# A DiT block on one NeuronCore: SiLU and gating of all attention pairs done in the output stage

## The chip, the core and the metric

One NeuronCore of a Trainium2 chip runs the whole program. The metric is device time in microseconds (us) of one execution; the time of a kernel is the median of its runs. A profile is one further execution taken with the hardware profiler; its times are counted from the start of the span. Engines are named as in the profile: PE (TensorE, matrix products), PEld (its weight loads), DVE (VectorE), ACT (ScalarE), POOL (GpSimd), SP (SyncE, which here only issues DMAs). ACT and POOL issue DMAs as well, each from its own queue and in its own instruction order.

## The reference, cut to what matters

One transformer layer on 1024 tokens of width 1024, with 256 context tokens. After an adaLN-modulated RMS norm, one projection gives eight groups of 512 columns. Half of the mixing width is attention, half a gated short convolution:

```python
q, k, v, za, u, bg, cg, zc = split(h @ w_in)
attn = neighbourhood_attention(q, k, v, kc, vc, rpb) * silu(za)
conv = bg * conv3(cg * u) * silu(zc)
x_new = x + gate * (concat([attn, conv]) @ w_out)
```

Attention has 8 heads of 64, here 4 pairs of heads with 128 channels each. Softmax is over a local window plus all context keys, so each head's output has to be divided by its row sums.

## The kernel before, in words

Everything is float32. To keep its precision, each product is done as three passes on high and low parts (`mm3`: high x high, high x low, low x high); each operand is split by a copy to the rounded type on ACT and a subtraction on DVE.

**Layout.** The mixed activations are kept with channels on partitions: eight blocks `f` of 128 channels by 1024 tokens. Blocks 0 to 3 are the attention pairs, 4 to 7 the convolution groups. Each goes through DRAM, in halves of 512 tokens (256 KB each).

**Stages.** (1) Norms and the first convolution group, to some 100 us. (2) The projections of q, k and v, to some 270 us. (3) Attention, to some 540 us: 36 steps (`quarter(n)`, four for a head), pipelined over each other. Into each step the generator `fill` puts two to four ticks of six products each, from the remaining projection units: first the units of `za` (`attn_group(f)`, one for each pair), then the convolution groups 1 to 3. The units' products are the rows `pu` of the profile. (4) The output stage, from 553 us: eight blocks times two halves of `w_out`, for eight tiles of 128 tokens; its products are the rows `pout`.

**Order.** In stage 3 the order of every engine's compute instructions and of the DMAs of SP is as written (`strict`, `behind`, L49 to L60); work that is put off is kept in two lists (`chore`, L301) and taken up at fixed places in the step. In stage 4 a scheduler orders the instructions of each engine. Engines take their instructions strictly in order, DMA issues too, so an issue that waits holds up what is behind it on that engine. A DMA issued by ACT or SP signals on one of eight completion counters, taken in turn by both, and it waits until the last transfer on its counter has landed.

**One attention step.** PE turns the running maxima (`pmx<-ci,mx`), DVE reduces them (`rm`), PE spreads the result (`pmx<-ci,rm`), ACT copies it (`mg`). PE does the scores of a new step (`pss`, `pc`). DVE subtracts the maxima, ACT takes two exponentials of each part (`phc`, `sc`, `phl`, `sb`), POOL and DVE form the low parts (`plc` on POOL, `pll` on DVE), PE multiplies by the values (`po`). DVE also adds the bias and updates the maxima (`mx`).

**SiLU and gate of a pair, before.** When both halves of the unit of `za` are done, `attn_group` has ACT take the SiLU of both out of PSUM, tile `zs` (`silus`, L477), and SP store them to `zs_d`. ACT's exponential and its SiLU need different tables, so ACT loads a table ahead of the two SiLUs and another ahead of the next exponential. When a pair's second head is done, its row sums and output lie in DRAM (`rs_d`, `o_d`; `finish`, L1035). For pairs 0 to 2, `gated(p)` (L1263) then advances by one piece in each step (L1081): SP loads the sums, DVE inverts them, SP stores them (`ri_d`); then for each half SP loads SiLU (`zs`), output (`tb`) and inverse sums (`rb`, two loads, each repeated over 64 partitions), DVE multiplies `zs` by `rb`, in a later step `tb` by `zs`, and SP stores the product to `y_d`. Pair 3 ends too late for that: `recip` (L498) inverts its sums and the output stage does its gate.

**Output stage, before.** For the blocks in the order `FORDER` = 4, 5, 6, 0, 1, 2, 3, 7, `put_y` loads `y_d` half by half, tile `tb` (four buffers of tag `zt`), and splits it: `yh` on ACT, `yl` on DVE. For block 3 it loads `zs` and `tb`, and two `rb` from POOL's queue, and does the two multiplications first. `load_wo` loads a half of a block of `w_out` (`woraw`, two buffers) and splits it into `woh` and `wol`. All these loads but `rb` are issued by ACT. PE first runs the six token tiles 0 to 5 of the first half of `w_out` through the blocks in turn, then the other tiles. `out_tile` multiplies by the gate (DVE), adds `x` (POOL) and stores.

Of the kernel before, what the change touches and what calls it, by code (L numbers as in the profile page):

```python
# [10 lines left out]
F32 = mybir.dt.float32  # L11
F32R = mybir.dt.float32r
BF16 = mybir.dt.bfloat16
AF = mybir.ActivationFunctionType
ALU = mybir.AluOpType
# [4 lines left out]
P = 128  # L20
D = 1024
T = 1024
# [5 lines left out]
NPAIR = NH // 2  # L28
NEG = -1.0e30
CTXT = 3  # L30
FORDER = [4, 5, 6, 0, 1, 2, 3, 7]
# [8 lines left out]
def body(tc, es, x, ctxt, w_ada, b_ada, w_in, q_g, k_g, rpbr, w_out, vecs, cst, out):  # L40
# [21 lines left out]
    pe, act, dve, pool = every = [ordered(e) for e in (nc.tensor, nc.scalar, nc.vector, nc.gpsimd)]  # L62
    sp = ordered(nc.sync)

    def sbuf(name, side=None, bufs=1):
        kw = {} if side is None else {"side": side}
        return tc.tile_pool(name=name, bufs=bufs, reuse_waits="tile", **kw)

    def psum(name):
        return tc.tile_pool(name=name, bufs=1, space=PSUM, reuse_waits="tile")  # L70
# [19 lines left out]
    def many(name, n, shape):  # L90
        return [dr.tile(shape, F32, name=f"{name}{i}")[:] for i in range(n)]
# [4 lines left out]
    o_d = many("o_d", NPAIR, [P, T])  # L96
    y_d = many("y_d", KT, [P, T])
    g_d = dr.tile([1, D], F32, name="g_d")
    rope_d = dr.tile([P, 2048], F32, name="rope_d")
    rs_d = many("rs_d", NPAIR, [2, 2, 512])  # L100
    zs_d = many("zs_d", NPAIR, [P, T])


    q_d = many("q_d", NH, [2, HD, 4, 2, 256])
# [46 lines left out]
    cvp = hs.enter_context(sbuf("cvp", side="right"))  # L151
# [149 lines left out]
    def chore(on_act=None, on_dve=None, queue=soon, frees=None):  # L301
        queue.append([on_act, on_dve, frees])
        if act not in strict:
            do_acts()
            do_dves()

    def do_acts():
        for c in soon + (slow if not any(c[1] and c[1].__name__ == "product" for c in soon) else []):
            if c[0]:
                c[0]()  # L310
                c[0] = None

    def do_dves(most=99):
        for queue in chores:
            while queue and not queue[0][0] and (queue is soon or most > 0 and not soon):
                on_dve = queue.pop(0)[1]
                if on_dve:
                    on_dve()
                    most -= 1
# [18 lines left out]
    def unit(col):  # L338

        w = ahead.pop(col, None)  # L340
        if w is None:
            w = []
            for r in loaded.pop(col, None) or unit_load(col):
                unit_split(r, w)
        nxt = follows.get(col)
        for half in range(2):
            cols = slice(half * 512, (half + 1) * 512)
            for k in range(KT):
                if k % 2 == 0:
                    yield None  # L350
                if k == 0:
                    while any(c[2] == half for c in slow):
                        do_acts()
                        do_dves()
                    ps = psm.tile([P, 512], F32, name="pu", tag="U", bufs=2)
                if k % 2 == 0:
                    tick = 4 * half + k // 2
                    if nxt and tick == 0:
                        raws = unit_load(nxt)
                    if nxt and tick in (3, 5):  # L360
                        unit_split(raws[tick // 5], ahead.setdefault(nxt, []))
                mm3(ps, *w[k], hh[k][:, cols], hl[k][:, cols], k == 0, k == KT - 1)
            yield half, ps

    def blocked(v):
        return v.rearrange("p (b r c) -> p b r c", b=4, r=16)

    def by_row(v):
        return v.rearrange("p (r b c) -> p b r c", r=16, b=4)
# [11 lines left out]
    def z_col(f):  # L381
        return CZA + f * P if f < 4 else CZC + (f - 4) * P
# [94 lines left out]
    def silus(z):  # L477
        out = []
        for half, ps in z:
            out.append(cvp.tile([P, 512], F32, name="zs", tag="ub", bufs=2))  # L480
            act.activation(out[half], ps, AF.Silu)
        return out

    def attn_group(f):

        z = []
        for got in unit(z_col(f)):
            if got:
                z.append(got)
            else:  # L490
                yield

        def on_act():
            for half, zs in enumerate(silus(z)):
                sp.dma_start(zs_d[f][:, half * 512:(half + 1) * 512], zs)
        chore(on_act)

    def recip(p, pl):  # L498

# [5 lines left out]
    def load_sums(f, half, rb, queue):  # L505
        for i in range(2):
            queue.dma_start(rb[64 * i:64 * i + 64],
                            ri_d[f][i:i + 1, half * 512:(half + 1) * 512].broadcast_to([64, 512]))
# [658 lines left out]
    for n in range(NT + 3):  # L1167


        p, t = divmod(n, NB)  # L1170
# [89 lines left out]

    gating = []

    def gated(f):  # L1263

        ri = ap.tile([P, 16], F32, name="ri", tag="ri", bufs=4)
        sp.dma_start(ri, rs_d[f].rearrange("h b (x c) -> (h b x) c", c=16))
        yield
        dve.reciprocal(ri, ri)
        sp.dma_start(ri_d[f].rearrange("h (x c) -> (h x) c", c=16), ri)
        yield  # L1270
        for half in range(2):
            cols = slice(half * 512, (half + 1) * 512)
            zs, tb, rb = (ap.tile([P, 512], F32, name=n, tag=n, bufs=1) for n in ("zs", "tb", "rb"))
            sp.dma_start(zs, zs_d[f][:, cols])
            sp.dma_start(tb, o_d[f][:, cols])
            load_sums(f, half, rb, sp)
            yield
            dve.tensor_tensor(zs, zs, rb, ALU.mult)
            yield
            dve.tensor_tensor(tb, tb, zs, ALU.mult)  # L1280
            sp.dma_start(y_d[f][:, cols], tb)

    with sbuf("att") as ap, psum("psb") as psb:
        sbank = psb.tile([P, 2, 512], F32, name="pss")
        strict[:] = every
        mx = ap.tile([P, T], F32, name="mx")
        sb_new = lambda: ap.tile([P, 2, 384], F32, name="sb", tag="sb", bufs=3)
        mg = ap.tile([P, T], F32, name="mg")
        heads[0].load_v()
        for n in range(4 * NH + 4):  # L1290
            h, g = divmod(n, 4)
            if 0 < h < NH and g == 0:
                heads[h].load_v()
            if h + 1 < NH and g:
                nx = heads[h + 1]
                for load in ((nx.masks, nx.load_q), (nx.load_k,), ())[g - 1]:
                    load()
            quarter(n)
            if ready:
                p = ready.pop()  # L1300
                if p < NPAIR - 1:
                    gating[:] = [gated(p)]
                else:
                    recip(p, ap)
        for _ in fill:
            do_dves()
            do_acts()
        while soon or slow:
            do_dves()
            do_acts()  # L1310
        strict[:] = []
# [5 lines left out]
    op = es.enter_context(sbuf("op"))  # L1317
# [2 lines left out]

    def load_wo(wp, nh, f):
        raw = op.tile([P, 512], F32, name="woraw", tag="woraw", bufs=2)
        act.dma_start(raw, w_out[0, f * P:(f + 1) * P, nh * 512:(nh + 1) * 512])
        wh = wp.tile([P, 512], F32R, name=f"woh{nh}{f}")
        wl = wp.tile([P, 512], F32R, name=f"wol{nh}{f}")
        act.copy(wh, raw)
        dve.tensor_tensor(wl, raw, wh[:].bitcast(F32), ALU.subtract)
        wo[nh, f] = wh, wl

    def put_y(yp, f):  # L1330

        yh = yp.tile([P, T], F32R, name=f"yh{f}")
        yl = yp.tile([P, T], F32R, name=f"yl{f}")
        for half in range(2):
            cols = slice(half * 512, (half + 1) * 512)
            tb = op.tile([P, 512], F32, name="tb", tag="zt", bufs=4)
            if f == NPAIR - 1:
                zs = op.tile([P, 512], F32, name="zs", tag="zt", bufs=4)
                rb = op.tile([P, 512], F32, name="rb", tag="rb", bufs=2)
                act.dma_start(zs, zs_d[f][:, cols])  # L1340
                act.dma_start(tb, o_d[f][:, cols])
                load_sums(f, half, rb, pool)
                dve.tensor_tensor(zs, zs, rb, ALU.mult)
                dve.tensor_tensor(tb, tb, zs, ALU.mult)
            else:
                act.dma_start(tb, y_d[f][:, cols])
            tv = blocked(tb[:]) if f < NPAIR else by_row(tb[:])
            act.copy(natural(yh[:], half), tv)
            dve.tensor_tensor(natural(yl[:], half), tv, natural(yh[:].bitcast(F32), half), ALU.subtract)
        y[f] = yh, yl  # L1350

    for f in FORDER[:-1]:
        put_y(op, f)
        load_wo(op, 0, f)
# [28 lines left out]
    for n, (nh, t) in enumerate([(0, 6), (0, 7)] + [(1, t) for t in range(NB)]):  # L1383
        ps = bank("pout", "US"[n % 2])
# [54 lines left out]
```

## Time and profile before

| | |
|---|---|
| median of 3 runs | 645.64 us (645.0 to 645.97) |
| the profiled execution: its time / its span | 646.57 us / 644.8 us |
| granted TensorE clock | 1.00 |
| PE busy, DVE busy, ACT busy, POOL busy | 98%, 67%, 50%, 20% of the span |
| bytes moved by DMA | 125.46 MB, mean 195 GB/s |
| DVE busy from 375 to 415 us | 37.25 of 40 us |
| PE busy from 544 to 584 us | 40.00 of 40 us |

A busy PE is not a PE at its peak here: matrix products overlap and their ends are modelled, so a wait of a few tenths of a us hides in a busy figure. Waits are read off the starts of successive products instead. Times in the views are us from the start of the span; a row of a timeline has start, length, engine, line, operation, tile written <- tiles read, and in brackets the idle time ahead of it with what ended it. L55 is the line of the helper that records ordered instructions, so these are told apart by their tiles.

### The profile page before, as it was taken

The page shows a single profiled execution, that of the slowest core. Times are in us where ns is not written, and L with a number is a line of the kernel's source. Part 1 is how long each engine was busy: PE and PEld are TensorE (multiplying, and loading weights), DVE is VectorE, ACT ScalarE, POOL GpSimd, SP SyncE. Part 2 cuts the span into 40 slices and gives each one's busy share as a digit, 9 for nine tenths or more (in the row PEclk, how much of TensorE's full clock was granted, in tenths as well). Part 3 has the DMA queues.
Part 4 walks back from the last instruction along what each step waited for, and adds up shares of the span by engine and source line. Part 5 has one row for each costly group of instructions (what it writes and reads, how often), then busy time and mean ns, then how long its engine had stood idle before and what let it go on. Part 6 is the DMA issues. An engine that isn't in the chain of part 4 may idle for free.

```text
span 644.8 us, 10300 instructions
## 1 busy us (share of the span) xinstructions
PE 629.4 (98%) x3479; PEld 537.3 (83%) x3480; DVE 432.9 (67%) x819; ACT 322.2 (50%) x692; POOL 130.3 (20%) x138
## 2 busy tenths in 40 slices
PE   8899999999999999999999999999999999999997
PEld 3477798999899999877878888888888888888885
DVE  1677746865775846557787889988998864575111
ACT  3666725533534543438776658565675545352000
POOL 1205003313223231102121111121111111004421
PEclk9999999999999999999999999999999999999999
DMA  8962556778795998799947768886872224976621
GB/s 325 374 227 104 134 186 196 213 219 233 215 278 148 279 267 236 194 236 216 230 114 209 188 149 204 209 211 154 220 166 76 79 79 118 307 236 206 199 98 53
DMA packets 118864, 125.46 MB, mean 195 GB/s; under 512 B 32817, under 2 KB 89353, under 8 KB 117532
## 3 DMA queue, kind: packets, MB, share of 16 engines
q1 hardware_dynamic: 112348, 113.23, 61.7%
q10 hardware_dynamic: 6208, 11.05, 5.8%
q0 software_dynamic: 256, 0.54, 0.3%
q8 instruction: 27, 0.44, 0.3%
q14 instruction: 25, 0.20, 0.1%
HBM read 88.01 MB, written 38.53 MB: 196 GB/s over the span
## 4 chain that ended last, share of the span: by engine, by line
PE 68%; DMA 9%; DVE 8%; ACT 6%; SPq 5%; issue 2%; POOL 2%; ACTq 0%; DVEq 0%; POOLq 0%
PE pu L55 18%; PE pacc L55 17%; PE po L55 5%; PE pout L76 5%; PE pout L75 5%; PE pout L74 4%; DMA v<-v_d 3%; DMA k_s<-k_d 3%; PE tr L55 3%; SPq L55 3%; PE cacc L55 3%; DVE mx L55 2%; PE acc L55 2%; PE pss L55 2%; PE pmx L55 2%
## 5 line engine op out<-in xcount | busy, mean ns | idle before, releaser
L55 PE MATMUL pu<-h,uh 128*128 128x512 f32 x544 | 169.0, 392 | 0.0
L55 PE MATMUL pacc<-wh,h 128*128 128x384 f32 x512 | 135.5, 338 | 0.0
L55 PEld LDWEIGHTS pu<-h,uh 128*128 128x128 f32 x544 | 98.2, 188 | 17.0
L55 PE MATMUL pu<-h,ul 128*128 128x512 f32 x272 | 106.4, 391 | 0.0
L55 PEld LDWEIGHTS pacc<-wh,h 128*128 128x128 f32 x512 | 92.8, 188 | 0.4 <-ACT qn L55 0.4
L55 POOL TENSOR_TENSOR plc<-sc,phc 128x512 fp32r<-128x512 f32 x32 | 42.5, 1330 | 221.1 <-ACT sc L55 99.2
L55 PE MATMUL pacc<-wl,h 128*128 128x384 f32 x256 | 85.6, 334 | 0.0
L55 POOL TENSOR_TENSOR ss<-ss,few 128x4 f32<-128x4 f32 (+1 forms) x40 | 41.9, 1050 | 127.8 <-DVE ss L55 127.4
L55 PEld LDWEIGHTS pu<-h,ul 128*128 128x128 f32 x272 | 51.1, 188 | 11.3
L55 DVE TENSOR_TENSOR mx<-mx,sb 128x384 f32<-128x384 f32 (+1 forms) x64 | 55.6, 877 | 2.0
L75 PE MATMUL pout<-wol,yh 128*128 128x512 f32 x128 | 49.8, 389 | 0.0
L76 PE MATMUL pout<-woh,yl 128*128 128x512 f32 x128 | 49.6, 389 | 0.0
L74 PE MATMUL pout<-woh,yh 128*128 128x512 f32 x128 | 48.3, 389 | 0.0
L55 PEld LDWEIGHTS pacc<-wl,h 128*128 128x128 f32 x256 | 48.1, 188 | 0.1
L55 DVE TENSOR_REDUCE ss<-sq 128x4 f32<-128x260 f32 (+1 forms) x40 | 15.8, 394 | 46.3 <-ACT sq L55 46.3
L55 ACT COPY mg<-pmx 128x256 f32<-128x256 f32 x32 | 12.0, 374 | 58.0 <-PE pmx L55 44.7
L55 ACT ACTIVATE sq<-pacc 128x256 f32<-128x256 f32 x32 | 12.3, 385 | 52.7 <-PE pacc L55 51.8
L1371 DVE TENSOR_TENSOR ot<-pout,gate 128x512 f32<-128x512 f32 x16 | 10.9, 689 | 38.3 <-PE pout L76 36.2
L55 DVE TENSOR_TENSOR pll<-sb,phl 128x768 fp32r<-128x768 f32 (+2 forms) x33 | 29.3, 889 | 7.6 <-ACT sb L55 7.6
L1372 POOL TENSOR_TENSOR ot<-ot,xr 128x512 f32<-128x512 f32 x15 | 20.1, 1351 | 67.9 <-DVE ot L1371 66.5
L55 DVE TENSOR_TENSOR sc<-sc,mg 128x512 f32<-128x512 f32 x32 | 21.8, 683 | 17.5 <-ACT mg L55 17.5
L55 ACT ACTIVATE qn<-pacc,ss 128x64 f32<-128x64 f32 x128 | 30.0, 329 | 6.3 <-POOL ss L55 3.2
(151 smaller groups left out, 1275.9 us busy)
## 6 DMA issues: line engine op xcount, KB each, us to landing
uraw<-in_w_in SPq DMA_DIRECT2D x34, 256.0 KB
q_d<-qs SPq DMA_DIRECT2D x64, 128.0 KB
k_s<-k_d SPq DMA_DIRECT2D x16, 512.0 KB
q_s<-q_d SPq DMA_DIRECT2D x32, 256.0 KB
wr<-in_w_in SPq DMA_DIRECT2D x40, 192.0 KB
slab<-in_w_ada SPq DMA_DIRECT2D x6, 1024.0 KB
t_d<-btw SPq DMA_DIRECT2D x8, 576.0 KB
bt<-t_d SPq DMA_DIRECT2D x8, 576.0 KB
```

Source lines behind the costliest of these rows:

```text
L55: i = emit(*a, **kw)
L74: i = pe.matmul(ps, ah, bh, start=first, stop=False)
L75: pe.matmul(ps, ah, bl, start=False, stop=False)
L76: pe.matmul(ps, al, bh, start=False, stop=last)
L1371: dve.tensor_tensor(ot, ps, gate[:, cols], ALU.mult)
L1372: (dve if (nh, t) == (1, NB - 1) else pool).tensor_tensor(ot, ot, xr, ALU.add)
```

## The change

`attn_group` no longer takes the SiLU: ACT copies each half of `za` out of PSUM as soon as it is done, and SP stores it raw to `z_d`. `gated` becomes `inverse`, which only inverts the sums of pairs 0 to 2. In the output stage `put_y` now treats all four pairs alike: it loads `z_d`, `o_d` and the inverse sums, ACT takes the SiLU in SBUF, DVE does the two multiplications, and then the split follows as before. The inverse sums of all pairs are loaded from POOL's queue, through two buffers. The tag `zt` has six buffers instead of four. The loads of blocks 1, 2, 3 and 7, and of their part of the first half of `w_out`, are issued by SP instead of ACT. `y_d` is now used by the convolution groups alone.

```diff
     def attn_group(f):
-        z = []
+        def keep(half, ps):
+            z = cvp.tile([P, 512], F32, name="z", tag="ub", bufs=2)
+            act.copy(z, ps)
+            sp.dma_start(z_d[f][:, half * 512:(half + 1) * 512], z)
+
         for got in unit(z_col(f)):
             if got:
-                z.append(got)
+                chore(lambda got=got: keep(*got))
             else:
                 yield
-
-        def on_act():
-            for half, zs in enumerate(silus(z)):
-                sp.dma_start(zs_d[f][:, half * 512:(half + 1) * 512], zs)
-        chore(on_act)
...
-    def gated(f):
+    def inverse(f):
         ri = ap.tile([P, 16], F32, name="ri", tag="ri", bufs=4)
         sp.dma_start(ri, rs_d[f].rearrange("h b (x c) -> (h b x) c", c=16))
         yield
         dve.reciprocal(ri, ri)
         sp.dma_start(ri_d[f].rearrange("h (x c) -> (h x) c", c=16), ri)
-        yield
-        for half in range(2):
-            cols = slice(half * 512, (half + 1) * 512)
-            zs, tb, rb = (ap.tile([P, 512], F32, name=n, tag=n, bufs=1) for n in ("zs", "tb", "rb"))
-            sp.dma_start(zs, zs_d[f][:, cols])
-            sp.dma_start(tb, o_d[f][:, cols])
-            load_sums(f, half, rb, sp)
-            yield
-            dve.tensor_tensor(zs, zs, rb, ALU.mult)
-            yield
-            dve.tensor_tensor(tb, tb, zs, ALU.mult)
-            sp.dma_start(y_d[f][:, cols], tb)
...
     def load_wo(wp, nh, f):
         raw = op.tile([P, 512], F32, name="woraw", tag="woraw", bufs=2)
-        act.dma_start(raw, w_out[0, f * P:(f + 1) * P, nh * 512:(nh + 1) * 512])
+        (act if nh or f in FORDER[:4] else sp).dma_start(raw, w_out[0, f * P:(f + 1) * P, nh * 512:(nh + 1) * 512])
...
     def put_y(yp, f):
...
-            tb = op.tile([P, 512], F32, name="tb", tag="zt", bufs=4)
-            if f == NPAIR - 1:
-                zs = op.tile([P, 512], F32, name="zs", tag="zt", bufs=4)
+            tb = op.tile([P, 512], F32, name="tb", tag="zt", bufs=6)
+            queue = act if f in FORDER[:4] else sp
+            if f < NPAIR:
+                zs = op.tile([P, 512], F32, name="zs", tag="zt", bufs=6)
                 rb = op.tile([P, 512], F32, name="rb", tag="rb", bufs=2)
-                act.dma_start(zs, zs_d[f][:, cols])
-                act.dma_start(tb, o_d[f][:, cols])
+                queue.dma_start(zs, z_d[f][:, cols])
+                queue.dma_start(tb, o_d[f][:, cols])
                 load_sums(f, half, rb, pool)
+                act.activation(zs, zs, AF.Silu)
                 dve.tensor_tensor(zs, zs, rb, ALU.mult)
                 dve.tensor_tensor(tb, tb, zs, ALU.mult)
             else:
-                act.dma_start(tb, y_d[f][:, cols])
+                queue.dma_start(tb, y_d[f][:, cols])
```

In the built programs, the instructions of PE, DVE and POOL up to the output stage stand in the same order, without the twelve multiplications on DVE. ACT has six table loads fewer (7 instead of 13) and, for each pair, a copy at two places where two SiLUs stood at one. In the output stage the scheduler gives another order: on PE a seventh token tile, and later an eighth, now stand among the products of the first six.

More of the change, by code (lines that the diff above doesn't have):

```diff
@@ L100, in body @@
     rs_d = many("rs_d", NPAIR, [2, 2, 512])
-    zs_d = many("zs_d", NPAIR, [P, T])
+    z_d = many("z_d", NPAIR, [P, T])
     q_d = many("q_d", NH, [2, HD, 4, 2, 256])
@@ L1301, in body @@
                 if p < NPAIR - 1:
-                    gating[:] = [gated(p)]
+                    gating[:] = [inverse(p)]
                 else:
```

## The prediction

> **What bounds the kernel now.** I read the page first, then the chain of waits, the timeline of PE around the steps that the chain names, and the table of windows for the output stage.
>
> ```profile
> span 644.8 us, 10300 instructions
> ...
> PE 629.4 (98%) x3479; PEld 537.3 (83%) x3480; DVE 432.9 (67%) x819; ACT 322.2 (50%) x692; POOL 130.3 (20%) x138
> ```
>
> PE is the bound: every other engine has idle time, and the kernel can only gain where PE waits. The change touches two stages, the attention (some 275 to 540 us) and the output stage (553 us to the end), so I ask where PE waits in the first, and whether it would wait in the second. In the chain, pieces of other engines stand between PE's where it waited:
>
> ```profile
> 318.78 1.28 ACT L55
> ...
> 392.44 0.68 DVE tb L55
> ...
> 553.28 1.59 PE pout L74 x7
> ```
>
> The first is a table load ahead of an exponential, the second one of the gating multiplications; both go. The third gives PE's pace in the output stage: 1.59 / 7 = 0.227 us for one product.
>
> **Part 1: what the attention gets back.** First a step in which nothing was late, then five in which something was:
>
> ```profile
> 467.02 0.39 PE L55 MATMUL pu<-h,ul 128*128 128x512 f32 x1
> 467.25 0.38 PE L55 MATMUL pmx<-ci,mx 128*128 128x128 f32 x2
> 467.39 0.48 PE L55 MATMUL po<-phc,v 128*65 128x256 f32 x2
> 467.70 0.28 PE L55 MATMUL po<-plc,v 128*65 128x256 f32 x1
> ...
> 468.06 0.28 PE L55 MATMUL po<-plc,v 128*65 128x256 f32 x1
> 468.17 0.41 PE L55 MATMUL pmx<-ci,rm 128*128 128x128 f32 x2
> ```
>
> ```profile
> 298.71 0.27 PE L55 MATMUL pmx<-ci,mx 128*128 128x128 f32 x1
> ...
> 299.71 0.48 PE L55 MATMUL po<-phc,v 128*65 128x256 f32 x2
> ...
> 300.38 0.28 PE L55 MATMUL po<-plc,v 128*65 128x256 f32 x1
> 300.83 0.43 PE L55 MATMUL pmx<-ci,rm 128*128 128x128 f32 x2 [0.17 <-DVE rm L55]
> ...
> 322.21 0.47 PE L55 MATMUL po<-phc,v 128*65 128x256 f32 x2
> 323.24 0.34 PE L55 MATMUL po<-plc,v 128*65 128x256 f32 x1 [0.57 <-POOL plc L55]
> ...
> 323.65 0.28 PE L55 MATMUL po<-plc,v 128*65 128x256 f32 x1
> 324.13 0.43 PE L55 MATMUL pmx<-ci,rm 128*128 128x128 f32 x2 [0.20 <-DVE rm L55]
> ...
> 345.39 0.28 PE L55 MATMUL po<-plc,v 128*65 128x256 f32 x1
> 345.84 0.43 PE L55 MATMUL pmx<-ci,rm 128*128 128x128 f32 x2 [0.17 <-DVE rm L55]
> ...
> 396.72 0.39 PE L55 MATMUL pu<-h,ul 128*128 128x512 f32 x1
> 397.25 0.41 PE L55 MATMUL pmx<-ci,mx 128*128 128x128 f32 x2
> ...
> 474.75 0.27 PE L55 MATMUL pmx<-ci,mx 128*128 128x128 f32 x1
> ...
> 475.29 0.47 PE L55 MATMUL po<-phc,v 128*65 128x256 f32 x2
> ```
>
> Read start to start. Undisturbed, the two `pmx` take 467.39 - 467.25 = 0.14, `po<-phc` to `po<-plc` 0.31, the last `plc` to `pmx<-ci,rm` 0.11, `pu` to `pmx` 0.23. So PE lost 1.00 - 0.14 = 0.86 at 298.7, 0.45 - 0.11 = 0.34 at 300.4, 1.03 - 0.31 = 0.72 at 322.2, 0.48 - 0.11 = 0.37 at 323.7, 0.45 - 0.11 = 0.34 at 345.4: together 2.63 us. These lie in the steps behind the three pairs' SiLUs that fall in the attention:
>
> ```profile
> L55 ACT ACT_TABLE_LOAD x13 | 16.7, 1283 | 1.0 <-PEq L1422 0.7
> ```
>
> ```profile
> L55 ACT ACTIVATE zs<-pu x16: 592/597/644, 130.6 to 542.4; 128x512 f32<-128x512 f32 x16
> ```
>
> Six loads of 1.28 go, 7.7 us of ACT, two around each pair. The SiLU itself only becomes a copy of the same 512 columns, which I cost at nothing. The load at 318.78 made the exponentials, and so `plc`, 1.28 later, more than the 0.72 lost there; at 298.7 the load ahead of the SiLUs delayed `mg`, and DVE's chain from it, by some 1.0 (an estimate: the load less the shift of one copy), more than 0.86. The other three are `rm` behind a late `pll` on the same chains.
>
> The remaining two, 0.53 - 0.23 = 0.30 at 396.7 and 0.54 - 0.14 = 0.40 at 474.8, wait for DVE's `mx`, and on DVE a gating multiplication stood 4 to 5 us earlier in the same step (392.44 above is one):
>
> ```profile
> L55 DVE TENSOR_TENSOR tb<-tb,zs 128x512 f32<-128x512 f32 x6 | 4.1, 685 | 0.0
> L55 DVE TENSOR_TENSOR zs<-zs,rb 128x512 f32<-128x512 f32 x6 | 4.1, 683 | 0.0
> ```
>
> Each that goes makes `mx` some 0.6 to 0.7 earlier. That gives 0.70 us, and the whole comes to 2.63 + 0.70 = 3.3 us. Two still smaller waits of the kind may come on top (0.4 at most, an estimate), and what is late next may take some back: with ACT and DVE ahead, `po` can wait for the loads of `v` and `k`, which issue no sooner than PE frees their buffers. The bounds are 1.6 (half) and 3.9; I take 3.3. All else there is free: SP has 30 DMAs fewer, the stores of `z_d` are as many and as large as those of `zs_d`, and the shorter hold of PSUM can only help.
>
> **Part 2: what the output stage has to do more.** It has all the work that left: 6 more SiLUs on ACT (6 x 0.60 = 3.6 us; the table is already SiLU's from the last convolution group), 12 more multiplications on DVE (8.2 us), 6 more loads of 256 KB, 12 more `rb` loads of 128 KB on POOL's queue, issued while POOL is idle.
>
> ```profile
> 544.00:560.00 16.00, 16.00 (x72) 13.23 (x72) 9.16 (x15) 5.84 (x10) 2.09 (x4) 1.00 1.00 321
> 560.00:568.00 8.00, 8.00 (x37) 6.64 (x36) 4.60 (x7) 4.65 (x9) 0.00 (x0) 1.00 0.84 275
> 568.00:576.00 8.00, 8.00 (x37) 6.61 (x36) 5.82 (x10) 2.85 (x5) 0.00 (x0) 1.00 0.76 231
> 576.00:584.00 8.00, 8.00 (x37) 6.62 (x36) 4.08 (x7) 3.63 (x7) 0.00 (x0) 1.00 0.47 146
> ```
>
> ```profile
> 578.29 0.69 DVE L1349 TENSOR_TENSOR yl<-tb,yh 128x512 fp32r<-128x512 f32 x1 [0.27 <-ACT yh L1348]
> ```
>
> After the stretch and its length stand the busy times of PE, PEld, DVE, ACT and POOL, the clock, the DMA share and GB/s. PE never waits here before the change. DVE has 23.7 of 40 us, ACT 17.0: there is room for 8.2 and 3.6. But the DMA is full, share 1.00, from 544 to 560; the last `yl` is ready at 579.0.
>
> *By bytes.* In the order of the changed program, 47 units of 256 KB are asked for from 542 up to pair 3's last load of `o_d` (9 for blocks 4, 5, 6 with their `w_out`, 7 for each of the four pairs, `rb` and `w_out` included, 7 for the gate row, the last convolution stores and `x`, 3 for block 7 and the second half of `w_out`). At 321 GB/s a unit takes 0.82: 544 + 47 x 0.82 = 582.5. At 275, for all that comes after 560 (27.4 units x 0.95), it is 586.1. PE's first product that needs pair 3 has 133 of the stage ahead of it, since the scheduler put two further tiles among the first six (before, it is 110): 553.3 + 133 x 0.227 = 583.5. From the landing to `yh` there are a multiplication and a copy, some 1.5 us with hand-overs. So PE waits 582.5 + 1.5 - 583.5 = 0.5 to 4.1 us, middle 2.3.
>
> The Trainium skill (DMA: Bandwidth & Descriptors, Issuing engines are not separate DMA queues) speaks against putting loads on SP's queue: DMAs started by different engines run on the same 16 engines, and a second issuer saves only issue time. The 1.00 above, with ACT, SP and POOL all issuing, agrees. The same page (Specifications) gives a limit of about 358 GB/s for the memory of a core; by it the 47 units would be in by 579 and PE would not wait, but the window holds 321 at a share of 1.00.
>
> *By the chain of buffers.* A half's load needs a free buffer of six, so it follows the work on the half three places ahead; latencies, from issue to use, are
>
> ```profile
> 549.80 0.34 ACTq L1346 DMA_DIRECT2D tb<-y_d  x1
> ...
> 557.34 0.62 ACT L1348 CAST yh<-tb 128x512 fp32r<-128x512 f32 x1 [3.30 <-DMA tb<-y_d]
> ...
> 567.56 0.34 ACTq L1323 DMA_DIRECT2D woraw<-in_w_out  x1
> ...
> 571.70 0.62 ACT L1326 CAST woh<-woraw 128x512 fp32r<-128x512 f32 x1 [3.14 <-DMA woraw<-in_w_out]
> ```
>
> ```profile
> DMA to landing us min/median/max: 3.9/4.2/4.8
> ```
>
> 7.5 while the DMA is full, 4.1 later, 4.2 for `rb`. Pair 0's loads issue at 549.8 to 552.4, when blocks 4 and 5 are split (as now), and land by 560.7; SiLU, two multiplications, copy and subtraction (0.60 + 2 x 0.68 + 0.62 + 0.69 = 3.3) make it 564, needed after 56 products at 566.0. Pair 1 starts at 557.8, when the first `o_d` of pair 0 has landed (the completion counter), and its last half is loaded from 562.5 and split at 571.5, needed after 84 at 572.4. Pair 2's `yh` stands on ACT behind the SiLU of pair 3, whose load waits for pair 1's second multiplication at 570.8: 570.8 + 4.1 = 574.9, and in order follow `yh` of the first half, `yl`, the next multiplication and the second `yh`, ready at 578.4, needed after 106 at 577.4. PE waits 1.0. Pair 3 is ready at 584.7, needed at 583.5 + 1.0: it costs 0.2 more. The chain thus gives 1.2, the bytes 2.3; they overlap rather than add, and I take the value between, 1.8 us. Below, it can be 0; above, with the 7.5 of the full DMA instead of 4.1 twice on this chain, 1.2 + 6.8 = 8.0.
>
> What is queued behind the waits: ACT holds `yh` and `woh` behind each SiLU, SP only further loads and the `x` rows that POOL needs from 587, so these do not decide.
>
> **Sum.** -3.3 + 1.8 = -1.5 us on a span of 644.8, so 643.3. The profiled execution took 646.57, so 645.1 there; it stands 0.93 above the median of 645.64, and the median to expect is 645.64 - 1.5 = 644.1.
>
> **Rivals.**
> *Starved output stage (slower).* Pairs 2 and 3 arrive late because six buffers and two for `rb` tie each load to work that itself waited for a load. For it: the share of 1.00 and the 7.5. Against it: the scheduler's tiles ahead of pairs 1 to 3, and a share of 0.84 and less from 560. Its price is a wait of 4.1 (bytes) to 8.0 (chain), middle 6.1: 645.6 - 3.3 + 6.1 = 648.4. It decides where pair 3's last load lands after 583.5 - 1.5 + 3.3 = 585.3 in the clock of before.
> *They cancel.* A gain of 2.7 (PE meets a later load, so that the two `rm` waits of 0.34 stay) and the bytes' wait of 2.3: 645.2, within 0.2%.
> *Cover holds (clearly faster).* With no wait in the output stage and 3.9 of gain: 641.7. For it: DVE and ACT have 16 and 23 us free there.
> That the change does not do what it says can be excluded: the six table loads and twelve multiplications are gone from the program of that stage.
>
> **How the numbers follow.** Forecast, 643.0 to 644.3: 0.36. Starved, 647 to 650, with its milder forms above 646.9: 0.35. Cancel: 0.19. Cover holds: 0.10. The forecast is the likeliest by little, and with the covered case it makes faster the likelier sign, so I stand with 644.1. Faster by over 0.2% 0.46, within 0.2% (about what a measurement of this kernel can tell from no change) 0.19, slower 0.35. Signs are open, so the range takes in most of both: 641.6 to 649.6. The forecast's own range is 642.5 to 645.
>
> **What would show it.** Right: 7 table loads; the pairs of rows at 298.7, 322.2, 396.7 and 474.8 at their undisturbed spacing; the first `pout` 3 us sooner; fewer than 2 us of gaps among the `pout` rows, ahead of pair 2 or 3. Wrong: the attention ends less than 1.6 us sooner (something else late, likely `mg` behind an issue on ACT, or `v`); gaps of more than 4 us, ahead of a product that needs `yh` of pair 2 or 3 or `woh` of a later tile; latencies of 6 us or more past 562.

## The result and the profile after

The changed kernel takes 648.51 us (median of 18 runs, 647.15 to 650.13), the kernel before 646.21 in runs beside them (18 runs, 645.0 to 651.1). The ratio is 1.0036, 95% interval 1.0024 to 1.0048: slower, by more than the 0.2% that can be told from no change. Forecast were 644.1 us and faster; the rival called the starved output stage stood at 648.4. The profiled execution took 648.31 us with a span of 646.5. One profile of an experiment (defer_x) ran at a granted clock of 0.75 throughout; it isn't read, and the kernel was profiled once more as defer_x2.

To see where the time went I measure two lengths in each trace, from starts of products on PE: the **attention** from its first `pss` to the first `pout`, and the **output stage** from the first to the last `pout`.

| kernel | attention against before | output stage against before | time (ratio to before, interval) |
|---|---|---|---|
| changed | -3.7 us | +6.9 us | 1.0036 (1.0024 to 1.0048) |

The rest of the difference of the two spans, -1.5 us, lies ahead of the attention, where nothing is changed; in the other traces below that part differs from before by -1.8 to +0.6, so it belongs to the executions. Without it the sum is +3.2; the medians say +2.3.

**The attention got what was forecast.** The page of the changed kernel, its tables, and the timeline of PE at the places that the prediction named (they come 1.5 to 2.0 us earlier now):

```profile
span 646.5 us, 10291 instructions
...
PE 629.2 (97%) x3479; PEld 538.4 (83%) x3480; DVE 437.3 (68%) x819; ACT 318.4 (49%) x694; POOL 136.7 (21%) x150
```

```profile
L55 ACT ACT_TABLE_LOAD x7 | 9.0, 1283 | 0.8 <-PEq L1411 0.7
```

```profile
297.18 0.38 PE L55 MATMUL pmx<-ci,mx 128*128 128x128 f32 x2
297.32 0.48 PE L55 MATMUL po<-phc,v 128*65 128x256 f32 x2
...
297.99 0.28 PE L55 MATMUL po<-plc,v 128*65 128x256 f32 x1
298.35 0.43 PE L55 MATMUL pmx<-ci,rm 128*128 128x128 f32 x2
...
319.64 0.30 PE L55 MATMUL pmx<-ci,mx 128*128 128x128 f32 x1
320.15 0.33 PE L55 MATMUL pmx<-ci,mx 128*128 128x128 f32 x1 [0.20 <-DVE mx L55]
320.25 0.46 PE L55 MATMUL po<-phc,v 128*65 128x256 f32 x2
320.55 0.28 PE L55 MATMUL po<-plc,v 128*65 128x256 f32 x1
```

From `pmx<-ci,mx` to `po` it is 0.14 again (0.86 more before the change), from `po<-phc` to `po<-plc` 0.30 (0.72 more before). Of the losses 0.25 is left at 297.99 to 298.35 and 0.47 at 319.64 to 320.25, the latter now ahead of `pmx` and for DVE's `mx`. Of the 13 table loads 7 are left.

**The output stage lost twice that.** PE's timeline there, then the windows (columns as in the prediction):

```profile
566.73 0.39 PE L76 MATMUL pout<-woh,yl 128*128 128x512 f32 x1
568.51 0.50 PE L74 MATMUL pout<-woh,yh 128*128 128x512 f32 x1 [1.40 <-ACT yh L1337]
...
571.84 1.75 PE L76 MATMUL pout<-woh,yl 128*128 128x512 f32 x7
576.54 1.02 PE L74 MATMUL pout<-woh,yh 128*128 128x512 f32 x2 [2.95 <-ACT woh L1313]
...
578.62 0.63 PE L75 MATMUL pout<-wol,yh 128*128 128x512 f32 x1
579.05 0.63 PE L74 MATMUL pout<-woh,yh 128*128 128x512 f32 x1
```

```profile
544.00:560.00 16.00, 16.00 (x72) 13.24 (x72) 10.29 (x17) 7.38 (x13) 2.07 (x4) 1.00 1.05 343
560.00:568.00 8.00, 7.12 (x32) 5.56 (x30) 3.75 (x7) 3.06 (x6) 2.07 (x4) 1.00 0.92 306
568.00:576.00 8.00, 5.08 (x21) 3.86 (x21) 5.75 (x9) 3.30 (x7) 2.07 (x4) 1.00 0.93 284
576.00:584.00 8.00, 7.43 (x24) 5.74 (x25) 6.66 (x11) 4.77 (x9) 0.00 (x0) 0.79 0.56 175
```

The product after 84 others reads pair 1's `yh` and comes 568.51 - 566.73 - 0.23 = 1.56 us late. The one after 105 comes 576.54 - (571.84 + 6 x 0.227) - 0.23 = 3.11 late: it reads `woh14`, a piece of the second half of `w_out` that the scheduler put ahead of pair 2, and pair 2's own `yh` was no earlier (the next product loses 0.30 more). Soon behind it come eight products 0.43 apart instead of 0.227, the clock of that window being 0.79: 8 x 0.2 = 1.6 us. 1.56 + 3.11 + 0.30 + 1.6 = 6.6, and the hand-overs behind each wait make the rest of the 6.9. The DMA share, which fell to 0.84 and 0.76 from 560 on before, now stays at 0.92 and more until 576.

What the late pieces waited for: issues on SP, the timelines of ACT and DVE, one row of the table of waits from 544 to 584, three of the chain of waits, and the landing times of the inverse sums:

```profile
554.81 0.39 SPq L1328 DMA_DIRECT2D zs<-z_d  x1
...
565.71 0.33 SPq L1328 DMA_DIRECT2D zs<-z_d  x1
...
567.83 0.32 SPq L1328 DMA_DIRECT2D zs<-z_d  x1
```

```profile
563.11 0.63 ACT L1331 ACTIVATE zs<-zs 128x512 f32<-128x512 f32 x1 [4.86 <-DMA zs<-z_d]
...
567.85 0.61 ACT L1337 CAST yh<-tb 128x512 fp32r<-128x512 f32 x1
...
572.18 0.63 ACT L1331 ACTIVATE zs<-zs 128x512 f32<-128x512 f32 x1 [2.66 <-DMA zs<-z_d]
572.71 0.60 ACT L1337 CAST yh<-tb 128x512 fp32r<-128x512 f32 x1
573.23 0.61 ACT L1313 CAST woh<-woraw 128x512 fp32r<-128x512 f32 x1
575.87 0.62 ACT L1313 CAST woh<-woraw 128x512 fp32r<-128x512 f32 x1 [2.03 <-DMA woraw<-in_w_out]
576.39 0.61 ACT L1337 CAST yh<-tb 128x512 fp32r<-128x512 f32 x1
```

```profile
559.84 0.69 DVE L1332 TENSOR_TENSOR zs<-zs,rb 128x512 f32<-128x512 f32 x1 [2.12 <-DMA rb<-ri_d]
564.39 0.69 DVE L1314 TENSOR_TENSOR wol<-woraw,woh 128x512 fp32r<-128x512 f32 x1 [3.86 <-ACT woh L1313]
565.00 0.69 DVE L1333 TENSOR_TENSOR tb<-tb,zs 128x512 f32<-128x512 f32 x1
```

```profile
POOL rb L506 <- DVE zs L1332: 26.2, 6, 12.2
```

```profile
552.12 7.05 DMA xr<-in_x
...
559.24 8.05 DMA woraw<-in_w_out
...
569.90 5.89 DMA woraw<-in_w_out
```

```profile
DMA to landing us min/median/max: 3.0/6.0/8.2
```

The row at 563.11 is the SiLU of pair 1's second half; its `z_d` load, issued at 554.81, took 8.3 us. On DVE the two multiplications of pair 1's first half (559.84, 565.00) stand 5.2 us apart, with a piece of `w_out` between them that waited for its own load; before them DVE waited 2.12 for `rb`. Pair 1's last `yh` (567.85) comes behind all this. In the chain a load of `w_out` is issued at 559.24, when a tile of x has landed, and takes 8.05. Pair 2's two `yh` (572.71, 576.39) stand behind pair 3's first SiLU and behind `woh14`. POOL waited 26.2 us, six times, for a multiplication to free one of two `rb` buffers, and the `rb` loads then took 6.0 us (4.2 before). The runs take up four suspects: the one product on `woh14`, ACT's order, the full DMA, and the buffers. DVE's order was not varied by itself.

### The profile page after: what moved, and what is told of

The parts are those of the page before. It is cut to its first block, busy times and chain, and to the rows that moved or that the text cites. A ratio compares the mean times of both kernels' runs of the same rounds, so it can differ in the third digit from the quotient of the medians.

```text
span 646.5 us, 10291 instructions
## 1 busy us (share of the span) xinstructions
PE 629.2 (97%) x3479; PEld 538.4 (83%) x3480; DVE 437.3 (68%) x819; ACT 318.4 (49%) x694; POOL 136.7 (21%) x150
## 4 chain that ended last, share of the span: by engine, by line
PE 72%; DMA 12%; DVE 5%; SPq 4%; ACT 3%; issue 1%; POOL 1%; ACTq 0%; DVEq 0%
PE pu L55 23%; PE pacc L55 17%; PE po L55 7%; PE pout L74 3%; PE pout L75 3%; PE pout L76 3%; SPq L55 3%; DMA woraw<-in_w_out 3%; DMA k_s<-k_d 3%; PE cacc L55 3%; PE pss L55 3%; PE pmx L55 2%; PE tr L55 2%; PE pc L55 2%; PE acc L55 1%
## 5 line engine op out<-in xcount | busy, mean ns | idle before, releaser
L55 DVE TENSOR_TENSOR mx<-mx,sb 128x384 f32<-128x384 f32 (+1 forms) x64 | 58.7, 926 | 2.0
L76 PE MATMUL pout<-woh,yl 128*128 128x512 f32 x128 | 46.4, 389 | 0.0
L74 PEld LDWEIGHTS pout<-woh,yh 128*128 128x128 f32 x128 | 24.6, 192 | 10.6 <-ACT woh L1313 3.4
L55 ACT COPY sc<-pc 128x512 f32<-128x512 f32 x32 | 18.8, 588 | 27.0 <-PE pc L55 27.0
```

What stands on the lines that cost most here:

```text
L55: i = emit(*a, **kw)
L74: i = pe.matmul(ps, ah, bh, start=first, stop=False)
L76: pe.matmul(ps, al, bh, start=False, stop=last)
```

## The experiments

All times are medians, with the ratio to runs of the kernel before made beside them.

**Attention alone (attn_alone).** Pairs 0 to 2 go into the output stage ungated.

```diff
-            if f < NPAIR:
+            if f == NPAIR - 1:
...
-                queue.dma_start(tb, y_d[f][:, cols])
+                queue.dma_start(tb, (o_d if f < NPAIR else y_d)[f][:, cols])
```

> The changed kernel's attention alone: pairs 0 to 2 are left ungated in the output stage (their o_d is loaded as it is, with no z_d, no inverse sums, no SiLU, no multiplications), pair 3 as in the changed kernel. Theory: the attention's gain of 3.7 us is real and the whole loss is the added work of the output stage: 646.2 - 3.7 = 642.5, no wait among the products of the output stage. Rival: the output stage, which starts 3.7 us sooner, meets loads that do not start as much sooner, and waits even without the added work: 644 to 646.

643.16 us, ratio 0.9938 (0.9914 to 0.9961). Attention -3.7, output stage 0.0. The windows show it without a wait:

```profile
560.00:568.00 8.00, 8.00 (x37) 6.61 (x36) 6.06 (x10) 4.69 (x9) 0.00 (x0) 1.00 0.83 282
568.00:576.00 8.00, 8.00 (x37) 6.62 (x36) 4.14 (x7) 3.22 (x6) 0.00 (x0) 1.00 0.30 100
```

The gain is real, and the whole loss comes with the added work of the output stage.

**SiLU in the attention, multiplications late (silu_early).** `attn_group` as before; in the output stage

```diff
-                act.activation(zs, zs, AF.Silu)
```

> The changed kernel, but SiLU taken in the attention as before (two SiLUs together, tables loaded around each pair, stored as zs_d); only the multiplications and the loads move to the output stage, without SiLU there. Theory: of the attention's gain 3.0 us belongs to the tables and 0.7 to the multiplications on DVE, so the first product of the output stage comes only 0.7 sooner than before; the output stage has the same loads and buffers and waits 3 to 7 us: 648.5 to 652.5. Rival, the multiplications are the larger part of the gain: first product 2 us or more sooner, time 646 to 648.

653.39 us, ratio 1.0106 (1.0078 to 1.0134). Attention -0.2, output stage +6.6. The timeline at the second of the places has the lateness of before, with 13 table loads:

```profile
322.53 0.46 PE L55 MATMUL po<-phc,v 128*65 128x256 f32 x2
323.55 0.33 PE L55 MATMUL po<-plc,v 128*65 128x256 f32 x1 [0.57 <-POOL plc L55]
```

So the tables are worth 3.5 of the 3.7 us, the twelve multiplications 0.2, not 0.7 (single traces). The output stage loses as much without the SiLUs: ACT's added SiLUs aren't the cause there.

**All loads from ACT's queue (act_queue).**

```diff
-            queue = act if f in FORDER[:4] else sp
+            queue = act
```

(and the same in `load_wo`).

> The changed kernel with all loads of the output stage on ACT's queue again (the SyncE queue undone). Theory: the queue itself decides little, because the loads wait for buffers and for the DMA engines, not for their issuer: 648.5, within 1 us. Rival 1, SyncE's queue costs, because its loads stand behind the x rows whose landing they wait for: 646 to 647.4. Rival 2, ACT's queue costs more, because a load then stands behind a SiLU that waits for its own load: 649.5 to 653.

648.96 us, ratio 1.0032 (1.0008 to 1.0056); attention -3.8, output stage +7.7. Undoing the queue changes nothing that the times can tell. This agrees with the Trainium skill (DMA: Bandwidth & Descriptors, Issuing engines are not separate DMA queues).

**The product on woh14 (hold8).** Each first product of a set of three from the second half of `w_out` is ordered behind the last product of the first six tiles.

```diff
+            i = out_mm(ps, nh, t, f)
+            if nh:
+                behind(i, last)
```

> The changed kernel, with all products of the second half of w_out held behind the last product of the first six token tiles. In the changed kernel's trace one such product (it reads woh14) stands ahead of pair 2's products, and PE waits 3.1 us for it at 573 us, after which ten products run at half the granted clock (2.2 us more). Theory A, this one product is the cause: both go, pair 1's wait of 1.6 stays: 646.2 - 3.7 (attention) + 1.6 = 644.1, faster than before. Theory B, the chain of buffers is late as a whole, so that PE only meets pair 2 or pair 3 instead: a wait of 3 to 5 us moves to pair 3's yh, 646.2 - 3.7 + 1.6 + 4 = 648.1, no better than the changed kernel (648.5).

650.16 us, ratio 1.0054 (1.0035 to 1.0073), output stage +7.4. Theory A fell. PE waits at the same place, now for pair 2's `yh`:

```profile
574.73 0.84 PE L76 MATMUL pout<-woh,yl 128*128 128x512 f32 x3
578.98 0.50 PE L74 MATMUL pout<-woh,yh 128*128 128x512 f32 x1 [3.41 <-ACT yh L1337]
```

**ACT's order (act_order), the kernel of hold8 with**

```diff
+                if done and not half:
+                    behind(i, done[-1])
...
+        if nh:
+            behind(i, done[-1])
```

where the first `i` is a pair's first SiLU, the second the split into `woh`, and `done` holds the pairs' `yh`.

> The kernel of hold8, with ACT's order in the output stage forced too: the first SiLU of a pair stands behind the last yh of the pair before, and the splits of the second half of w_out behind the last yh of pair 3. Theory T2 (ACT's order): pair 1's wait of 1.6 stays, pair 2's yh is ready some 3.8 us sooner, so that its wait and the half clock behind it go, and pair 3 waits 0 to 2: 644 to 646. Theory T1 (the DMA): the loads are as late as before, and the wait of 3 us or more appears ahead of pair 2 or 3 again: 648 to 650.

651.82 us, ratio 1.0081 (1.0055 to 1.0108), output stage +7.9. Pair 2's wait fell to 1.6 us, and pair 3 got one:

```profile
581.78 0.39 PE L76 MATMUL pout<-woh,yl 128*128 128x512 f32 x1
585.10 0.50 PE L74 MATMUL pout<-woh,yh 128*128 128x512 f32 x1 [2.94 <-ACT yh L1342]
```

T2 fell as well, for the part of ACT's order that the edit forces. Two edits in a row only moved the wait, which points at the loads themselves.

**Gate row and x tiles later (defer_x, defer_x2, one kernel).**

```diff
-    sp.dma_start(gate, g_d.broadcast_to([P, D]))
+    behind(sp.dma_start(gate, g_d.broadcast_to([P, D])), last_y[0])
...
-        sp.dma_start(xr, x[0, rows, cols])
+        behind(sp.dma_start(xr, x[0, rows, cols]), last_y[0])
```

> The changed kernel, with the loads of the gate row (512 KB) and of the first three x tiles (256 KB each) issued by SP behind the last load of blocks 0 to 7, instead of between 549 and 555 us. Theory T1, the full DMA makes the pairs late: 1.28 MB less ahead of them is 4 us at 321 GB/s, so pair 1's wait of 1.6 us goes, the wait ahead of pair 2 falls from 3.1 to 0 to 1.5, and with it the half clock behind it (2.2 us): 642.5 to 644.5. Theory T2, the order of ACT makes pair 2 late (its second yh stands behind pair 3's first SiLU and behind woh14, both of which wait for loads that wait for buffers): only pair 1's wait goes: 646 to 647.5.

> The kernel of defer_x once more, for a profile at full clock (that of defer_x ran at a granted clock of 0.75 throughout). The output stage is 6.9 us longer than before in the changed kernel, 4.6 with more buffers for rb alone, 0.7 with both edits. T1 and T3 as separate causes: the gate row and x tiles alone take away 2 to 4, a wait of 3 to 5 us with the half clock behind it is left at pair 2 or 3; 646 to 648. If the two together are needed for any gain, as links of one chain: 6 to 7 us stay lost, 648 to 649.

647.81 and 647.75 us, ratios 1.0012 (0.9991 to 1.0032) and 1.0018 (1.0 to 1.0035); in the trace, output stage +4.1. Pair 1's wait is gone; one of 2.0 is left ahead of `woh14`, with the half clock behind it:

```profile
571.40 0.39 PE L76 MATMUL pout<-woh,yl 128*128 128x512 f32 x1
573.66 1.02 PE L74 MATMUL pout<-woh,yh 128*128 128x512 f32 x2 [1.87 <-ACT woh L1313]
...
575.24 0.63 PE L75 MATMUL pout<-wol,yh 128*128 128x512 f32 x1
```

The edit takes bytes out of the pairs' way and also frees the completion counters that the tiles of x held (in the changed kernel SP waited 1.5 us at 559.24 for one). These two aren't separated here.

**The edits of defer_x and act_order together (defer_order).** The latter holds that of hold8.

> Both edits together (gate row and x tiles later, ACT's order forced, the second half of w_out held). If T1 and T2 each hold for their part, PE has no wait in the output stage and the attention's gain is left: 646.4 - 3.7 = 642.7, faster than both kernels. If a third cause (the two buffers of rb or of woraw) holds the pairs back, a wait of 1 to 4 us is left: 643.7 to 648.

648.81 us, ratio 1.0032 (1.0013 to 1.005), output stage +5.0: only pair 3 waits, and a further cause shows, on PE, DVE and POOL:

```profile
576.02 1.75 PE L76 MATMUL pout<-woh,yl 128*128 128x512 f32 x7
580.86 0.50 PE L74 MATMUL pout<-woh,yh 128*128 128x512 f32 x1 [3.09 <-ACT yh L1342]
```

```profile
577.52 0.69 DVE L1337 TENSOR_TENSOR zs<-zs,rb 128x512 f32<-128x512 f32 x1 [2.83 <-DMA rb<-ri_d]
```

```profile
570.86 1.03 POOL L506 DMA_DIRECT2D rb<-ri_d  x2 [2.52 <-DVE zs L1337]
```

The multiplication waits for an `rb` that was issued only when an older one was used up, some 6 us before.

**More buffers for rb (rb4, defer_rb4, defer_order_rb4).**

```diff
-                rb = op.tile([P, 512], F32, name="rb", tag="rb", bufs=2)
+                rb = (rp if f else op).tile([P, 512], F32, name="rb", tag="rb", bufs=4 if f else 2)
```

with the pool `rp` opened ahead of the loop; alone, with defer_x, and with defer_order.

> The changed kernel with four more buffers for the inverse sums: rb of pairs 1 to 3 has four of its own instead of sharing two with pair 0; nothing else is edited (the order that the scheduler gives changes with it: the first product of the second half of w_out then stands behind pair 3's first). Theory T3, the two buffers of rb hold pairs 2 and 3 (a load is issued only when the multiplication two halves before is done, and lands 5.4 to 7.1 us later while the DMA is full): pair 1's wait of about 1.5 stays (T1), those ahead of pairs 2 and 3 go with the half clock: 646.4 - 3.7 + 1.5 = 644.2, up to 645.5. Rival, the full DMA alone (T1): the earlier rb loads only push the other loads back, 647.5 to 649.5.

> Gate row and first x tiles later (as in defer_x) and four more buffers for rb; ACT's order not forced. T1 and T3 together: no wait at pair 1 and 2, at most 1 us at the product that reads woh14 ahead of pair 3: 642.7 to 644. If ACT's order (T2) matters beside them: 645 to 647.

> The kernel of defer_order (gate row and x tiles later, ACT's order forced, the second half of w_out held) with four more buffers for rb. There pair 3 alone waited, 3.25 us, for a multiplication whose rb landed 6.1 us after an issue that waited for a buffer. T3: this wait and the half clock behind it (1.6 us) go, and the attention's gain is left: 642.7, 641.8 to 643.7, faster than both kernels. Rival, the transfers are late whatever the buffers (T1 alone): 645.5 to 648.8, as without them.

rb4: 647.49 us, ratio 1.001 (0.9995 to 1.0025), output stage +4.6. The time came out at the rival's lower end, and the trace has waits of 0.5 to 1.3 us at pairs 0, 1 and 2 and one of 1.0 at a later piece of `w_out`: eight `rb` loads now go out at once at 550 and land up to 10.1 us later, ahead of the others. defer_rb4: 645.53, ratio 0.9977 (0.996 to 0.9994), output stage +0.7, no wait among the first six tiles. defer_order_rb4: 645.54, ratio 0.9989 (0.997 to 1.0009), output stage +0.6, so the part of ACT's order that act_order forces doesn't matter beside them. The windows of defer_rb4:

```profile
560.00:568.00 8.00, 8.00 (x37) 6.64 (x36) 5.67 (x10) 4.50 (x8) 2.06 (x4) 1.00 0.97 311
568.00:576.00 8.00, 8.00 (x37) 6.63 (x36) 7.51 (x13) 4.70 (x8) 0.00 (x0) 1.00 0.94 299
576.00:584.00 8.00, 8.00 (x37) 6.62 (x36) 3.46 (x6) 2.29 (x4) 0.00 (x0) 1.00 0.62 221
```

The DMA is as full as in the changed kernel, but what PE needs first goes out first: the load of pair 1's second half is issued 4.1 us behind the first `pout` (553.43 - 549.34) instead of 6.9 (554.81 - 547.91), and pair 1's last `yh` starts 16.4 us behind it (565.74) instead of 19.9 (567.85). The output stage's loss over the two edits is thus 6.9 (none), 4.1 (gate row and x later), 4.6 (more `rb`), 0.7 (both): they take 2.8 and 2.3 alone, 6.2 together. With other buffers the scheduler also gives another order. On PE the `woh14` product goes behind pair 3's first; hold8 shows that this alone gains nothing. On ACT pair 1's first `yh` goes ahead of its second SiLU, and on DVE its first two multiplications follow each other (561.04 and 561.77 in defer_rb4) with no piece of `w_out` between. This part of the order isn't separated from the buffers here. defer_rb4 is faster than the changed kernel, and than the kernel before by 0.2%, about what can be told, though its median gained 1.6 us (645.53 against 647.13) where its span lost 3.1; that profile was among its fastest runs.

**Four buffers of zt (zt4).**

```diff
-            tb = op.tile([P, 512], F32, name="tb", tag="zt", bufs=6)
+            tb = op.tile([P, 512], F32, name="tb", tag="zt", bufs=4)
```

(`zs` alike).

> The changed kernel with four buffers of tag zt instead of six, as many as before. If the buffers of the pairs' loads bind beside those of rb, each load is issued a half later still and PE waits longer: output stage 10 us or more longer than before, 651 to 656. If rb's buffers and the DMA alone bind: 648 to 650, as the changed kernel.

651.12 us, ratio 1.0073 (1.0049 to 1.0097), but +6.7 in the trace, as with six; the wait stands earlier, at pair 1:

```profile
567.76 0.84 PE L76 MATMUL pout<-woh,yl 128*128 128x512 f32 x3
572.37 0.80 PE L74 MATMUL pout<-woh,yh 128*128 128x512 f32 x1 [3.77 <-ACT yh L1337]
573.39 0.63 PE L74 MATMUL pout<-woh,yh 128*128 128x512 f32 x1
```

The times say that the kernel with four is the slower one, the trace doesn't show it, and the order changes with the buffers here too: what two more buffers are worth stays open.

## Why the prediction was wrong, point by point

- **Part 1, 3.3 us: right** in sum, 3.7 measured. Its split was off: tables 3.5 instead of 2.6, multiplications 0.2 instead of 0.7.
- **Part 2, 1.8 us: the step that failed**, with 6.9 measured. The failure is in the chain of buffers, which gave 1.2. Moved by the 5.2 us by which the first `pout` came sooner, the chain's dates are 566.3, 573.2 and 579.5 for the last `yh` of pairs 1, 2 and 3; measured are 568.5, 577.0 and 583.1, later by 2.2, 3.8 and 3.6. Two of its terms were wrong.
  - *The latencies*, "7.5 while the DMA is full, 4.1 later, 4.2 for `rb`", were read in a stage without the added loads, though the same part adds 6 loads of 256 KB and 12 of 128 KB to it. With them the share stays at 0.92 and above until 576, the load of pair 1 took 8.3 us and `rb` 6.0. The 4.1 was nearly right: pair 3's first load took 4.4 (567.83 to 572.18), but it went out at 567.83, 2.2 behind the date of 570.8 - 5.2.
  - *What queues behind a wait* was put at nothing ("so these do not decide" names ACT and SP, and DVE not at all). Pair 1's last `yh` ended 5.4 us after its last SiLU began (563.11 to 568.5), where the prediction's own steps between the two, 0.60 + 2 x 0.68 + 0.62, make 2.6. In between DVE worked off what had stood behind a piece of `w_out` since 560.5, and SP's next loads for pairs 2 and 3 went out only as the second multiplications of pair 1's halves ended (565.71, 567.83). How much of the 6.9 is DVE's order stays open.
- **The buffers of `rb` and the pieces of `w_out` were left out of the chain**, which followed `zt` alone. In defer_order, pair 3's multiplication waits for an `rb` that POOL issued late; with more buffers, and the order that comes with them, its 5.0 becomes 0.6 (defer_order_rb4).
- **Slack was read as safety.** Pair 1 was dated 571.5 against a need of 572.4, and so costed at nothing; 0.9 us of slack on a chain with an 8 us load cost 1.56.
- **The cover had needs of its own.** The 133 products ahead of pair 3 were counted as cover, but some read `woh14` and `woh15`, whose loads pass through two buffers behind the same pairs. hold8 shows that this cost nothing beyond the pairs' lateness, only that it covered nothing.
- **ACT's waits and SP's queue "do not decide": right as far as it was tried**, for a pair's first SiLU and the splits of the second half of `w_out` on ACT (act_order, defer_order_rb4), and for loads issued by ACT instead of SP (act_queue).
- **The half clock behind a long wait, 1.6 us, was in no term.**
- **The bytes** gave the transfers as a whole, 0.5 to 4.1 us of waiting; they say nothing of the order within the stage, and there, 1.28 MB that nobody needed until 591.4, the first multiplication by the gate, went ahead of the pairs (defer_x2, 2.8 us).
- **The rival was right**: late pairs 2 and 3 from buffers tied to loads, priced at 6.1; that pair 1 would be late too was neither in it nor in the forecast. The value between the two middles, 1.8, was taken as if the stage had the DMA of before; the upper bound, "the 7.5 of the full DMA instead of 4.1 twice", came near the size of what happened.

## What to carry to other kernels

Don't take a load's latency from a stage to which the change adds loads: here `rb` went from 4.2 to 6.0 us, and each buffer that ties a load to earlier work repeats the difference. Date the queue of every engine that a wait stops, not only the loads of the tile in question. When work moves behind a full DMA, put what is needed last (here a gate row and tiles of x) behind what is needed first, and give the smallest tile of the chain enough buffers too; either alone brought less than half of what both did. When a wait only moves as its order is mended, as in hold8 and act_order, look at what the loads behind it wait for.

## What the runs showed of the hardware

In these traces the products behind a longer gap on PE run at half pace. Gaps between starts of 1.8 and 2.1 us (act_order and act_queue, pairs 2 and 1) were followed by products 0.23 apart, gaps of 2.26 (defer_x2) to 4.2 us (zt4) by products 0.427 apart, at once (zt4) or up to 1.7 us behind the gap, for 3.3 to 5.2 us. The Trainium skill (TensorE: Matmul & The Clock Gate, What's actually happening) puts the half rate behind an idle window of about 3.4 us; the 0.427 agrees, but here 2.26 us from start to start, 1.87 of them idle, were enough.
